# Five feed-forward stages: first weights by plain loads, the others further ahead

## The chip, the cores and the metric

One core of a Trainium2 chip runs the kernel. The metric is the device time of one execution, in microseconds (us). An engine's instructions run in the order in which the program issues them; the engines are PE (matrix products), DVE (vector operations), ACT (activations and copies), POOL (GpSimd) and SP (which issues most of the DMAs).

## The reference

Two network blocks on x of 512 tokens by 1024 features, in float32. What the change touches are the five feed-forward stages; each reads the normed residual stream and adds to it (factor 0.5 in the first four, 1.0 in the fifth). Between them lie the two mixers of the first block and the mixer of the second, which stay as they are.

```python
def _swiglu(x, w_gate, w_up, w_down):
    hid = jax.nn.silu(jnp.einsum('bsd,df->bsf', x, w_gate)) * jnp.einsum('bsd,df->bsf', x, w_up)
    return jnp.einsum('bsf,fd->bsd', hid, w_down)

for l in range(DEPTH):            # DEPTH = 2
    h = h + 0.5 * _swiglu(_rmsnorm(h, ffn1_norm[l]), ffn1_w_gate[l], ffn1_w_up[l], ffn1_w_down[l])
    h = h + _hybrid_mixer(_rmsnorm(h, mix_norm[l]), ...)
    h = h + 0.5 * _swiglu(_rmsnorm(h, ffn2_norm[l]), ffn2_w_gate[l], ffn2_w_up[l], ffn2_w_down[l])
# second block: a mixer, then h = h + (silu(gate) * up) @ w_ffn_out, then the final norm
```

D_MODEL is 1024 and D_FF 2816, so a stage has 22 hidden blocks of 128 for gate and 22 for up.

## The kernel before

**Data.** The residual stream lies transposed in SBUF as eight tiles `h0` to `h7` of 128x512 (features by tokens). For float32 accuracy each operand is split into a high and a low part, `split` or `parts_of`: ACT copies the source to fp32r (`...h`, `whi`), DVE subtracts (`...l`, `wlo`). Each product of a weight and an x tile is then three matmuls.

**A feed-forward stage** (`ffn`, L508) is made in pairs of hidden blocks, 22 pairs, gate and up in turn. A pair of output blocks by pairs of input blocks is a 2x2 matrix product, and it is done with seven products `a` to `g` (`product`, L451) instead of eight, with sums of weight tiles and of x tiles: `halves` (L420) makes the x operands in four blocks (each from two h tiles: on ACT `xe`, `sq`, `bh`, `nh`, `xo`, `sq`, `nh`, `bh`, `th`), and `prepare` (L391) the weights. One product is 12 matmuls of 128x256: 4 blocks, three each. `steps` (L489) gives the order of the products: both products that need only the first weights, a and c, lead each pair. Three PSUM banks per pair, `pX`, `pW`, `pV`, hold a-d-e-g, c-f and b.

**Weights.** A pair's four 128x512 tiles a11, a21, a22, a12 lie side by side in `wq`, a quad. `load_quad` (L378) loads columns 0 to 1023 into `wsum`, 0 to 511 into `wa` and 1024 to 2047 into `wrest`, all from SP, and then POOL issues a DMA that adds columns 512 to 1535 onto `wsum`: its halves become a11+a21 (for e) and a21+a22 (for c). It must wait for the plain `wsum` to land. The sum for d is made by POOL (`ws`, L406), those for f by DVE (L411). `wsum`, `wrest` and the split tiles of 128x1024 share a pool of 12 buffers (`wpool`) with the streamed weights of the mixers and of the down products (`wraw`, split to `whi` and `wlo`); the tiles of 128x512 are in a pool of 63 (`slots`).

**When.** Quads are loaded, and products prepared, LEAD = 8 products ahead in the program (L531). The first two quads of a stage are loaded by `ahead` (L499) before the stage begins: in the constructor for stage 0, in the last quarter of a mixer or of the feed-forward stage before for the others. A scheduler fixes each engine's order of instructions at build time; buffers and semaphores then decide when each one runs. The down products (`pd`, L241 to L243, matmuls of 128x512) of a part of the hidden blocks are run twice within a stage (ENDS), after pairs 3 and 7 of gate and up, and a third time at its end; L526 adds their result to h.

## Time and profile before

| | us |
|---|---|
| median of three runs | 3457.65 (3455.81 to 3466.18) |
| profiled execution | 3456.21 |
| its span | 3454.4 |
| around the span | 1.8 |
| PE busy | 3201.6 |
| DVE busy | 2445.0 |
| ACT busy | 1535.8 |
| POOL busy | 703.2 |

The span is the time from the first instruction to the last. "Busy" leaves out waiting. In a list of waits a row names the waiting engine and tile, and the instruction that came last of those it waited for; in a timeline the bracket behind an instruction gives the idle time before it and what ended that. The mean granted clock of PE is 0.972 of full speed over the run.

### The profile page before, as it was taken

How to read it: one execution, taken by the hardware profiler on the slowest of the kernel's cores; microseconds unless marked ns; L12 is line 12 of the kernel's file. 1: busy time of each engine (PE TensorE's matmuls, PEld its weight loads, DVE VectorE, ACT ScalarE, POOL GpSimd, SP SyncE). 2: the span in 40 equal slices, each digit the busy share in tenths (PEclk: the TensorE clock that was granted, in tenths of full speed). 3: DMA queues.
4: the chain of work that ended last, by engine and by line, in shares of the span. 5: the costliest groups of instructions: out<-in, count | busy, mean ns of one | idle time of the engine just before them, and what ended most of it. 6: DMA issues, size and time to landing. Idle time of an engine off the chain costs nothing. (4 is left out here: it accounts for less than half of the span.)

```text
span 3454.4 us, 48230 instructions
## 1 busy us (share of the span) xinstructions
PE 3201.6 (93%) x18602; PEld 2757.8 (80%) x18602; DVE 2445.0 (71%) x4094; ACT 1535.8 (44%) x2586; POOL 703.2 (20%) x799
## 2 busy tenths in 40 slices
PE   4999999987999799999899799999999999999999
PEld 4998877767998698887777698887777777879888
DVE  6855778657765785767866685667788887568565
ACT  5533534335533453434333453355444366355343
POOL 2211124212111121111431221122111133122111
PEclk9999999998999899999999899999999999999999
DMA  5655332124654374533222274533333222347452
GB/s 141 172 143 136 94 96 75 45 86 104 162 147 125 104 177 130 149 100 98 72 60 82 74 181 133 145 89 107 92 98 104 87 81 74 115 116 177 130 148 83
DMA packets 142470, 391.39 MB, mean 113 GB/s; under 512 B 22176, under 2 KB 38688, under 8 KB 142240
## 3 DMA queue, kind: packets, MB, share of 16 engines
q1 hardware_dynamic: 126400, 330.64, 31.1%
q0 software_dynamic: 15840, 57.68, 10.1%
q8 instruction: 145, 2.38, 0.3%
q14 instruction: 85, 0.70, 0.1%
HBM read 384.85 MB, written 2.88 MB: 112 GB/s over the span
## 5 line engine op out<-in xcount | busy, mean ns | idle before, releaser
L203 DVE TENSOR_TENSOR wlo<-wraw,whi 128x1024 fp32r<-128x1024 f32 x306 | 389.7, 1278 | 117.7 <-ACT whi L202 60.5
L202 ACT ACTIVATE whi<-wraw 128x1024 fp32r<-128x1024 f32 x306 | 320.7, 1052 | 325.2 <-DMA wraw<-ws 293.7
L241 PE MATMUL pd<-hidh,whi 128*128 128x512 f32 x880 | 348.4, 396 | 8.6 <-ACT whi L202 8.6
L243 PE MATMUL pd<-hidh,wlo 128*128 128x512 f32 x880 | 348.2, 396 | 1.2 <-DVE wlo L203 1.2
L242 PE MATMUL pd<-hidl,whi 128*128 128x512 f32 x880 | 347.9, 395 | 0.0
L526 DVE SCALAR_TENSOR_TENSOR h<-pd,h 128x512 f32<-128x512 f32 x120 | 82.7, 689 | 343.2 <-PE pd L243 343.1
L406 POOL TENSOR_TENSOR ws<-wsum,wrest 128x512 f32<-128x512 f32 x110 | 173.7, 1582 | 649.3 <-DMA wsum<-wq 355.3
L465 PE MATMUL pX<-th,whi 128*128 128x256 f32 x880 | 251.4, 286 | 5.4 <-DVE oq L480 3.7
L465 PE MATMUL pX<-tl,whi 128*128 128x256 f32 x880 | 249.4, 283 | 0.0
L465 PE MATMUL pX<-th,wlo 128*128 128x256 f32 x880 | 249.1, 283 | 0.0
L388 POOL DMA_DIRECT2D wsum<-wq x110 | 96.7, 879 | 718.5 <-DMA wsum<-wq 553.4
L241 PEld LDWEIGHTS pd<-hidh,whi 128*128 128x128 f32 x880 | 166.1, 189 | 45.6 <-ACT whi L202 9.0
L243 PEld LDWEIGHTS pd<-hidh,wlo 128*128 128x128 f32 x880 | 166.0, 189 | 40.9 <-DVE wlo L203 2.9
L243 PE MATMUL pj<-x,wlo 128*128 128x512 f32 x476 | 192.8, 405 | 5.9 <-DVE wlo L203 5.9
L242 PEld LDWEIGHTS pd<-hidl,whi 128*128 128x128 f32 x880 | 166.1, 189 | 37.2
L243 PE MATMUL pj<-xh,wlo 128*128 128x512 f32 x476 | 191.5, 402 | 3.2 <-DVE wlo L203 3.2
L241 PE MATMUL pj<-x,whi 128*128 128x512 f32 x476 | 193.2, 406 | 0.8 <-ACT whi L202 0.4
L241 PE MATMUL pj<-xh,whi 128*128 128x512 f32 x476 | 191.1, 401 | 3.1 <-ACT whi L202 3.1
L242 PE MATMUL pj<-xl,whi 128*128 128x512 f32 x476 | 190.4, 400 | 2.0 <-DVE xl L307 2.0
L242 PE MATMUL pj<-x,whi 128*128 128x512 f32 x476 | 191.5, 402 | 0.0
L202 ACT ACTIVATE whi<-wsum 128x1024 fp32r<-128x1024 f32 x110 | 115.6, 1051 | 162.6 <-DMA wsum<-wq 162.6
L203 DVE TENSOR_TENSOR wlo<-wsum,whi 128x1024 fp32r<-128x1024 f32 x110 | 146.9, 1336 | 50.3 <-ACT whi L202 49.7
(456 smaller groups left out, 9643.4 us busy)
## 6 DMA issues: line engine op xcount, KB each, us to landing
wraw<-ws SPq DMA_DIRECT2D x306, 512.0 KB
wsum<-wq SPq DMA_DIRECT2D x110, 512.0 KB
wrest<-wq SPq DMA_DIRECT2D x110, 512.0 KB
wsum<-wq POOLq DMA_DIRECT2D x110, 512.0 KB, 7.3
wa<-wq SPq DMA_DIRECT2D x110, 256.0 KB
csb<-drow SPq DMA_DIRECT2D x32, 256.0 KB
bc<-drow SPq DMA_DIRECT2D x24, 256.0 KB
tab<-tables SPq DMA_DIRECT2D x15, 256.0 KB
```

Of the source, the lines that this page charges most:

```text
L202: self.nc.scalar.activation(hi, src, AF.Copy)
L203: self.nc.vector.tensor_tensor(lo, src, hi.bitcast(F32), ALU.subtract)
L241: nc.tensor.matmul(ps, lhsT=wh, rhs=xh, start=st, stop=False)
L242: nc.tensor.matmul(ps, lhsT=wh, rhs=xl, start=False, stop=False)
L243: nc.tensor.matmul(ps, lhsT=wl, rhs=xh, start=False, stop=en)
L388: nc.gpsimd.dma_start(w.sums, src[:, 512:1536], accum_op=ALU.add)
L406: nc.gpsimd.tensor_tensor(w.s2, w.sums[:, lo], w.rest[:, lo], ALU.add)
L465: nc.tensor.matmul(ps, lhsT=a[:, j * P:(j + 1) * P], rhs=b, start=p in "acb" and j + i == 0, stop=j == len(xs) - 1 and i == 2, skip_group_ ...
L526: nc.vector.scalar_tensor_tensor(self.h[mm], pds[mm], factor, self.h[mm], ALU.mult, ALU.add)
```

## The change

The first two quads of each stage are loaded as four plain tiles of 256 KB each (`early_tile`, into `slots`) in place of the plain and the accumulating DMAs; DVE adds what has to be summed (`prepare_early`), and each of the seven weights is split by itself. Other quads are loaded 16 products ahead, prepared 8 ahead as before. In the constructor, h tiles and weight tiles alternate in order of use, a small tile of gains (`gain0`) comes first, and cols and the constants come behind. The first two pairs of stage 0 begin with a, c and b together, block of x by block of x (`opening`), 72 matmuls. `ealog` is made in the first mixer. The 110 accumulating DMAs become 100.

```diff
--- before.py
+++ after.py
@@ -158,17 +158,19 @@
         self.tiny = pool("tiny", 4)
         self.psum = pool("psum", 1, space=bass.MemoryType.PSUM)
         self.dram = pool("dram", 2, space=bass.MemoryType.DRAM)
+        self.gain0 = self.const.tile([P, KB], F32, name="gain0")
+        nc.sync.dma_start(self.gain0, a["cols"][:, 0:KB])
+        self.h = [self.hpool.tile([P, S], F32, name=f"h{k}") for k in range(KB)]
+        self.ahead(start=True)
+        g, u = self.first
+        for t in ("h0", (g, 0), (u, 0), "h2", (g, 1), (g, 2), "h4", (u, 1), (u, 2), "h6", "h1", (g, 3), "h3", (u, 3), "h5", "h7"):
+            if isinstance(t, str):
+                k = int(t[1:])
+                nc.sync.dma_start(self.h[k], a["xT"][:, k])
+            else:
+                self.early_tile(*t)
         self.cols = self.const.tile([P, NCOL], F32, name="cols")
         nc.sync.dma_start(self.cols, a["cols"])
-        self.ealog = self.const.tile([P, DEPTH + 1], F32, name="ealog")
-        nc.scalar.activation(self.ealog, self.cols[:, COLS["alog"]:COLS["alog"] + DEPTH + 1], AF.Exp)
-        self.h = []
-        for k in range(KB):
-            t = self.hpool.tile([P, S], F32, name=f"h{k}")
-            nc.sync.dma_start(t, a["xT"][:, k])
-            self.h.append(t)
-            if k == 1:
-                self.ahead()
         self.cst = self.const.tile([P, len(CONSTS), P], F32, name="cst")
         nc.sync.dma_start(self.cst, a["consts"])
 
@@ -179,6 +181,8 @@
         return self.c(name).unsqueeze(1).to_broadcast([P, n, P])
 
     def col(self, name, i=0, rows=slice(0, P)):
+        if name == "ffn1_0":
+            return self.gain0[rows, i:i + 1]
         j = COLS[name] + i
         return self.cols[rows, j:j + 1]
 
@@ -388,11 +392,39 @@
         nc.gpsimd.dma_start(w.sums, src[:, 512:1536], accum_op=ALU.add)
         return w
 
+    def load_early(self, key):
+
+        q = len(self.quads)
+        self.quads.append(key)
+        return type("Early", (), dict(raw={}, src=self.a["wq"][q], part={}, s={}))
+
+    def early_tile(self, w, i):
+        w.raw[i] = self.slot("wr")
+        self.nc.sync.dma_start(w.raw[i], w.src[:, 512 * i:512 * i + 512])
+
+    def prepare_early(self, w, p):
+        add = lambda name, a, b: (w.s.setdefault(name, self.slot("ws")), self.nc.vector.tensor_tensor(w.s[name], a, b, ALU.add))[0]
+        a11, a21, a22, a12 = (w.raw[i] for i in range(4))
+        if p == "c":
+            t = add("c", a21, a22)
+        elif p == "d":
+            t = add("d", w.s["c"], a11)
+        elif p == "e":
+            t = add("e", a11, a21)
+        elif p == "f":
+            self.prepare(w, "d")
+            t = add("f", a12, w.s["d"])
+        else:
+            t = {"a": a11, "b": a12, "g": a22}[p]
+        w.part[p] = self.split(t, "we")
+
     def prepare(self, w, p):
 
         nc = self.nc
         if p in w.part:
             return
+        if hasattr(w, "raw"):
+            return self.prepare_early(w, p)
         lo, hi = slice(0, 512), slice(512, 1024)
         if p == "a":
             w.part["a"] = self.split(w.a11, "wa")
@@ -448,22 +480,37 @@
             xs.append(x)
         return xs, acc
 
+    def matmuls(self, m, p, j, x, last):
+
+        bank = "X" if p in "adeg" else "W" if p in "cf" else "V"
+        if p in "acb" and j == 0:
+            m.ps[bank] = self.ps(f"p{bank}", tag="mm" if bank == "X" else "mx")
+        wh, wl = m.w.part[p]
+        xh, xl = x[p]
+        for i, (a, b) in enumerate(((wh, xh), (wh, xl), (wl, xh))):
+            self.nc.tensor.matmul(m.ps[bank][:, 0:HT], lhsT=a[:, j * P:(j + 1) * P], rhs=b, start=p in "acb" and j + i == 0,
+                                  stop=last and i == 2, skip_group_check=True)
+
+    def opening(self, ms, ps, xs):
+
+        for j, x in enumerate(xs):
+            for p in ps:
+                for m in ms:
+                    self.matmuls(m, p, j, x, j == len(xs) - 1)
+        for p in ps:
+            for m in ms:
+                self.taken(m, p)
+
     def product(self, m, p, xs):
 
 
-        nc = self.nc
-        self.prepare(m.w, p)
-        wh, wl = m.w.part[p]
-        bank = "X" if p in "adeg" else "W" if p in "cf" else "V"
-        if p in "acb":
-            m.ps[bank] = self.ps(f"p{bank}", tag="mm" if bank == "X" else "mx")
+        for j, x in enumerate(xs):
+            self.matmuls(m, p, j, x, j == len(xs) - 1)
+        self.taken(m, p)
+
+    def taken(self, m, p):
+        nc = self.nc
         X, W, V = (m.ps[b][:, 0:HT] if b in m.ps else None for b in "XWV")
-        ps = m.ps[bank][:, 0:HT]
-        for j, x in enumerate(xs):
-            xh, xl = x[p]
-            for i, (a, b) in enumerate(((wh, xh), (wh, xl), (wl, xh))):
-                nc.tensor.matmul(ps, lhsT=a[:, j * P:(j + 1) * P], rhs=b, start=p in "acb" and j + i == 0,
-                                 stop=j == len(xs) - 1 and i == 2, skip_group_check=True)
         lo, hi = slice(0, HT), slice(HT, S)
         if p == "a":
             m.snap = self.slot("snap")
@@ -486,21 +533,30 @@
             nc.vector.scalar_tensor_tensor(o[:, lo], X, -1.0, m.r[:, lo], ALU.mult, ALU.mult)
             nc.vector.scalar_tensor_tensor(o[:, hi], m.o2[:, hi], -1.0, m.r[:, hi], ALU.mult, ALU.mult)
 
-    def steps(self, n):
+    def steps(self, n, first):
 
         s = lambda *t: [(i, p) for i, ps in t for p in ps]
-        yield s((0, "ac"), (1, "ac"), (0, "db"), (1, "d"), (0, "e"))
-        yield s((2, "ac"), (0, "fg"), (1, "eb"), (2, "d"), (1, "fg"))
+        if first:
+            yield [(i, p) for p in "acb" for i in range(2)]
+            yield s((0, "d"), (1, "d"), (0, "e"), (2, "ac"), (0, "fg"), (1, "e"), (2, "d"), (1, "fg"))
+        else:
+            yield s((0, "ac"), (1, "ac"), (0, "db"), (1, "d"), (0, "e"))
+            yield s((2, "ac"), (0, "fg"), (1, "eb"), (2, "d"), (1, "fg"))
         for i in range(3, n):
             yield s((i, "ac"), (i - 1, "eb"), (i, "d"), (i - 1, "fg"))
         yield s((n - 1, "be"))
         yield s((n - 1, "fg"))
 
-    def ahead(self):
+    def ahead(self, start=False):
 
         names, l = FFNS[self.stage]
         self.stage += 1
-        self.first = [self.load_quad((names[i], l, 0)) for i in range(2)]
+        self.first = [self.load_early((names[i], l, 0)) for i in range(2)]
+        if start:
+            return
+        for i in range(4):
+            for w in self.first:
+                self.early_tile(w, i)
         for p in "ac":
             for w in self.first:
                 self.prepare(w, p)
@@ -512,10 +568,11 @@
         for m, w in zip(pairs, self.first):
             m.w = w
         self.first = None
-        steps = list(self.steps(n))
+        start = gain == "ffn1_0"
+        steps = list(self.steps(n, start))
         flat = [t for s in steps for t in s]
         xs, acc = self.halves(gain)
-        done, hid, part, due = 0, [], [], None
+        done, hid, part, due, r = 0, [], [], None, None
 
         def down(blocks, ks, first=True, last=True):
             for mm in blocks:
@@ -527,12 +584,18 @@
 
         pds = {}
         for k, step in enumerate(steps):
+            if start and k == 0:
+                for i, p in step:
+                    self.prepare(pairs[i].w, p)
+                self.opening(pairs[:2], "acb", xs)
+                done, step = len(step), []
             for i, p in step:
-                for j, q in flat[done:done + LEAD]:
+                for j, q in flat[done:done + 2 * LEAD]:
                     if pairs[j].w is None:
                         pairs[j].w = self.load_quad(pairs[j].key)
+                for j, q in flat[done:done + LEAD]:
                     self.prepare(pairs[j].w, q)
-                if done == 4:
+                if r is None and done >= 4:
                     r = self.slot("R")
                     self.rsqrt(r, self.total(acc), 1.0 / DM, self.slot)
                     for m in pairs:
@@ -662,6 +725,9 @@
 
     def mixer1(self, l, nxt):
         nc = self.nc
+        if l == 0:
+            self.ealog = self.const.tile([P, DEPTH + 1], F32, name="ealog")
+            nc.scalar.activation(self.ealog, self.cols[:, COLS["alog"]:COLS["alog"] + DEPTH + 1], AF.Exp)
         xs, r, total = self.norm(f"mix_{l}")
         m = type("Mix", (), dict(l=l, xs=xs, r=r, y=[]))
         ps = self.proj(("small", l), xs)
```

**Place 1: ACT at the start of stage 0.** Before, from its first weight: `wah` and `whi` are the first two quads' weights, `xe` to `th` the x blocks.

```order
L253 ACTIVATE wah_97<-wa_84 128x512
L202 ACTIVATE whi_105<-wsum_83 128x1024
L253 ACTIVATE wah_101<-wa_91 128x512
L435 ACTIVATE xe_129<-h0_79,cols_75 128x512
L313 ACTIVATE sq_140<-h0_79 128x512
L417 ACTIVATE bh_127<-xe_129 128x256
L202 ACTIVATE whi_109<-wsum_90 128x1024
L417 ACTIVATE nh_133<-n_131 128x256
L440 ACTIVATE xo_130<-h1_81,cols_75 128x512
```

Now, from the middle of the first x block: 

```order
L449 ACTIVATE nh_119<-n_117 128x256
L472 ACTIVATE xo_116<-h1_78,gain0_75 128x512
L317 ACTIVATE sq_134<-h1_78 128x512
L730 ACTIVATE ealog_3984<-cols_109 128x3
L449 ACTIVATE nh_119<-n_117 128x256
L449 ACTIVATE bh_123<-xo_116 128x512
```

the second half of the second x block:

```order
L472 ACTIVATE xo_148<-h3_80,gain0_75 128x512
L317 ACTIVATE sq_168<-h3_80 128x512
L206 ACTIVATE whi_407<-wsum_371 128x1024
L449 ACTIVATE nh_151<-n_149 128x256
L449 ACTIVATE bh_155<-xo_148 128x512
L206 ACTIVATE whi_538<-wsum_378 128x1024
L449 ACTIVATE th_153<-t_150 128x512
L467 ACTIVATE xe_183<-h4_81,gain0_75 128x512
```

and the end of the fourth:

```order
L449 ACTIVATE th_223<-t_220 128x512
L257 ACTIVATE weh_251<-wr_86 128x512
L257 ACTIVATE weh_255<-wr_88 128x512
L257 ACTIVATE weh_261<-ws_259 128x512
L257 ACTIVATE weh_267<-ws_265 128x512
L257 ACTIVATE weh_271<-wr_102 128x512
```

The first two quads' weights (now `weh`) stood ahead of and inside the first x block and now stand behind the fourth. `ealog`, which reads cols, stands in the first block, and two `whi` of the third and fourth quads (wsum_371, wsum_378) in the second.

**Place 2: DVE where the first part's down products begin in stage 0** (`h0` is the first result added to h; the `wlo<-wrest` next to it belongs to a product f). Before:

```order
L548 TENSOR_TENSOR o_1507<-o_1507,o_1645 128x512
L526 SCALAR_TENSOR_TENSOR h0_79<-pd_1710,h0_79 128x512
L203 TENSOR_TENSOR wlo_1597<-wsum_1570,whi_1596 128x1024
L254 TENSOR_TENSOR wdl_1651<-ws_1648,wdh_1650 128x512
L203 TENSOR_TENSOR wlo_1669<-wrest_1434,whi_1668 128x1024
L486 SCALAR_TENSOR_TENSOR o_1646<-pX_1443,R_361 128x256
```

Now:

```order
L533 SCALAR_TENSOR_TENSOR o_1681<-pX_1478,R_427 128x256
L207 TENSOR_TENSOR wlo_1632<-wsum_1443,whi_1631 128x1024
L611 TENSOR_TENSOR o_1542<-o_1542,o_1680 128x512
L207 TENSOR_TENSOR wlo_1704<-wrest_1313,whi_1703 128x1024
L258 TENSOR_TENSOR hidl_1744<-o_1542,hidh_1743 128x512
L611 TENSOR_TENSOR o_1543<-o_1543,o_1681 128x512
L258 TENSOR_TENSOR hidl_1749<-o_1543,hidh_1748 128x512
L583 SCALAR_TENSOR_TENSOR h0_77<-pd_1752,h0_77 128x512
L258 TENSOR_TENSOR wal_2003<-wa_1584,wah_2002 128x512
```

Both `wlo` of the pairs in work stood behind the addition to h0 and now stand ahead of it. The nine other places of this kind (two in each stage) differ in the same way.

**Place 3: ACT at the start of the third stage (ffn1 of layer 1, from about 1150 us)**, behind the stage before it; `whi<-wraw` are weights of that stage's last down products. Before, from within the first x block on:

```order
L417 ACTIVATE nh_11269<-n_11267 128x256
L202 ACTIVATE whi_11163<-wsum_11141 128x1024
L417 ACTIVATE th_11271<-t_11268 128x512
L202 ACTIVATE whi_11167<-wsum_11148 128x1024
L435 ACTIVATE xe_11297<-h2_113,cols_75 128x512
L313 ACTIVATE sq_11308<-h2_113 128x512
L417 ACTIVATE bh_11263<-xe_11297 128x256
L417 ACTIVATE nh_11301<-n_11299 128x256
L440 ACTIVATE xo_11298<-h3_115,cols_75 128x512
L313 ACTIVATE sq_11318<-h3_115 128x512
L417 ACTIVATE nh_11301<-n_11299 128x256
L202 ACTIVATE whi_11174<-wraw_11172 128x1024
```

Now, from the last weights ahead of the first x block on:

```order
L257 ACTIVATE weh_11219<-wr_11201 128x512
L257 ACTIVATE weh_11225<-ws_11223 128x512
L206 ACTIVATE whi_11238<-wraw_11236 128x1024
L257 ACTIVATE weh_11231<-ws_11229 128x512
L467 ACTIVATE xe_11329<-h0_77,cols_109 128x512
L317 ACTIVATE sq_11340<-h0_77 128x512
L449 ACTIVATE bh_11327<-xe_11329 128x256
L206 ACTIVATE whi_11270<-wraw_11268 128x1024
L449 ACTIVATE nh_11333<-n_11331 128x256
L472 ACTIVATE xo_11330<-h1_78,cols_109 128x512
```

The `whi` of two down products stood in the second and third x blocks, behind `whi` that wait for accumulates, and now stand ahead of the first block and inside it; the four `weh` of the first two quads' a and c stand ahead of the x blocks.

## Rows read from the trace of the kernel before

**Rows 1.** the page, parts 1 (busy us, share, instructions) and 6 (us to landing)

```profile
PE 3201.6 (93%) x18602; PEld 2757.8 (80%) x18602; DVE 2445.0 (71%) x4094; ACT 1535.8 (44%) x2586; POOL 703.2 (20%) x799
...
wsum<-wq POOLq DMA_DIRECT2D x110, 512.0 KB, 7.3
```

**Rows 2.** PE's waits, whole run: engine, line, awaited instruction: us, times, longest

```profile
PE pX L465 <- ACT bh L417: 53.8, 6, 21.4
PE pV L465 <- ACT wbh L253: 23.2, 5, 5.3
PE pW L465 <- DVE wlo L203: 22.4, 15, 2.0
...
PE pd L241 <- ACT whi L202: 10.6, 2, 8.6
```

**Rows 3.** PE's timeline, 160 to 172 us: start, us, instruction, [idle before <- releaser]

```profile
171.13 0.38 PE L465 MATMUL pW<-bh,wlo 128*128 128x256 f32 x1 [2.00 <-DVE wlo L203]
```

**Rows 4.** DVE's timeline, 160 to 173 us

```profile
167.52 0.69 DVE L526 SCALAR_TENSOR_TENSOR h<-pd,h 128x512 f32<-128x512 f32 x1 [3.78 <-PE pd L243]
168.13 1.22 DVE L203 TENSOR_TENSOR wlo<-wsum,whi 128x1024 fp32r<-128x1024 f32 x1
169.26 0.68 DVE L254 TENSOR_TENSOR wdl<-ws,wdh 128x512 fp32r<-128x512 f32 x1
169.86 1.22 DVE L203 TENSOR_TENSOR wlo<-wrest,whi 128x1024 fp32r<-128x1024 f32 x1
```

**Rows 5.** PE's timeline, 0 to 64 us

```profile
21.39 0.79 PE L465 MATMUL pX<-bh,wah 128*128 128x256 f32 x2 [21.39 <-ACT bh L417]
...
63.05 0.39 PE L465 MATMUL pX<-th,whi 128*128 128x256 f32 x1 [0.35 <-ACT snap L472]
```

**Rows 6.** ACT's timeline, 0 to 66 us

```profile
18.32 1.06 ACT L202 ACTIVATE whi<-wsum 128x1024 fp32r<-128x1024 f32 x1 [8.70 <-DMA wsum<-wq]
...
19.80 0.71 ACT L435 ACTIVATE xe<-h,cols 128x512 f32<-128x512 f32 x1
...
27.81 0.71 ACT L435 ACTIVATE xe<-h,cols 128x512 f32<-128x512 f32 x1
...
37.36 0.71 ACT L435 ACTIVATE xe<-h,cols 128x512 f32<-128x512 f32 x1
...
45.73 0.71 ACT L435 ACTIVATE xe<-h,cols 128x512 f32<-128x512 f32 x1
...
55.27 0.63 ACT L417 ACTIVATE th<-t 128x512 fp32r<-128x512 f32 x1 [3.89 <-DVE t L446]
```

**Rows 7.** POOL's timeline, 0 to 60 us

```profile
8.63 1.00 POOL L388 DMA_DIRECT2D wsum<-wq  x1 [8.18 <-DMA wsum<-wq]
...
50.08 4.54 POOL L406 TENSOR_TENSOR ws<-wsum,wrest 128x512 f32<-128x512 f32 x3
```

**Rows 8.** busy us (count) of PE, PEld, DVE, ACT, POOL; clock, DMA share, GB/s

```profile
15.00:20.00 5.00, 0.00 (x0) 0.00 (x0) 0.59 (x1) 1.68 (x3) 0.00 (x0) 1.00 1.06 252
20.00:25.00 5.00, 3.12 (x11) 2.62 (x12) 3.89 (x7) 4.24 (x9) 0.85 (x1) 1.00 1.02 399
55.00:63.00 8.00, 5.61 (x24) 5.11 (x24) 4.64 (x7) 3.90 (x8) 0.00 (x0) 0.57 0.00 0
63.00:75.90 12.90, 12.85 (x108) 12.85 (x108) 8.52 (x14) 10.53 (x18) 0.88 (x1) 1.00 0.55 124
```

**Rows 9.** ACT's timeline, 1150 to 1204 us

```profile
1153.62 0.72 ACT L435 ACTIVATE xe<-h,cols 128x512 f32<-128x512 f32 x1 [5.76 <-DVE h L526]
...
1165.00 1.06 ACT L202 ACTIVATE whi<-wsum 128x1024 fp32r<-128x1024 f32 x1 [3.55 <-DMA wsum<-wq]
...
1190.17 1.06 ACT L202 ACTIVATE whi<-wsum 128x1024 fp32r<-128x1024 f32 x1 [3.64 <-DMA wsum<-wq]
...
1198.76 0.63 ACT L417 ACTIVATE th<-t 128x512 fp32r<-128x512 f32 x1 [5.49 <-DVE t L446]
```

**Rows 10.** PE's timeline, 1150 to 1216 us

```profile
1171.18 0.79 PE L241 MATMUL pd<-hidh,whi 128*128 128x512 f32 x1 [8.61 <-ACT whi L202]
```

## What the change does to the time: the prediction

> **What bounds the kernel now.** I read the page first: PE is busy 3201.6 us of the 3454.4 us span [rows 1], so 252.8 us of idle PE are all that better loading could return. The list of PE's waits over the whole run then says whom it idles for [rows 2]. Look there for two kinds. Four of the rows belong to the openings of the five feed-forward stages: `bh`, an operand half of x, costs 53.8 us in 6 waits; `wbh`, the first weight after the x blocks, 23.2 us in 5; a `whi` of a down product 10.6 us in 2. The fourth kind is in mid-stage: products on bank W wait for `wlo`, 22.4 us in 15 waits, none above 2.0 us.
>
> The timelines tell what these waits are. In mid-stage, PE stands 2.00 us at 171.13 us [rows 3]. The reason is on DVE [rows 4]: it stood 3.78 us for the last matmul of the first down block (`h<-pd` at 167.52), and three subtractions lay behind it in its order, two `wlo` and a `wdl`; the `wlo` that PE wants comes last, from 169.86 to 171.08. This is a matter of order on DVE; no transfer is late by then. It happens where a part's down products begin, twice in each stage: 10 x 2.0 = 20.0 us of the 22.4 us, which leaves 2.4 us for five small ones.
>
> In stage 0, PE begins at 21.39 us and reaches the eighth product (84 matmuls done) at 63.05 [rows 5]. Between the two, ACT paces it [rows 6]: it first stands 8.70 us for a summed weight tile, then passes the four x blocks, which begin at 19.80, 27.81, 37.36 and 45.73, and the last `th` comes at 55.27: 8.0 to 9.5 us a block.
>
> **The change part by part.** *Order at a part's first down product.* Loading 16 products ahead leaves the scheduler a summed tile early enough to put its subtractions before the addition to h: in the new DVE order both `wlo` stand ahead of `h0`, and the same in all ten places. In the new order the second `wlo` follows the end of a pX product by four DVE instructions, 0.4 + 1.22 + 0.68 + 1.22 = 3.5 us by like rows [rows 4]; PE has 24 matmuls of 128x512 and 12 of 128x256 to do meanwhile, 36 x 0.119 us at the least = 4.3 us (the 0.119 below). So nothing should be late. Between 0 and all of it, I take **-20 us**; bounds -22.4 and 0.
>
> *Stage 0.* The first weights now come plainly, without the accumulate that took from 8.63 [rows 7] to 18.32 us [rows 6]. But ACT's new order does not use that. `ealog` stands inside the first x block and waits for cols, which is queued behind sixteen tiles of 256 KB: 4.2 MB at the 252 to 399 GB/s of these microseconds [rows 8] are 10.5 to 16.6 us, so about 12 to 18 us from the start; I take 17, since the two first x rows must share with weights. Two `whi` of the third and fourth quads stand in the second block and wait for accumulates that are issued behind all this: plain tiles at about 21 us, then 7.3 (the median landing [rows 1]) to 9.7 us each; I take 30 and 36 us. Blocks three and four follow at 8.0 to 9.5 us each, and all six first weights come after the last `th`. So the last `th` comes at about 36 + 1.7 + 2 x 8.4 = 54.5, as late as before (55.27), and PE's first matmul moves from 21.39 to about 55 us. The opening's 72 matmuls were half done by then before. Now they run after it: the first 28 at a low clock (0.57 granted in 55 to 63 us, mostly the lower of its two levels, 1.2 GHz: 0.21 us each), the rest at 12.85 us / 108 = 0.119 us [rows 8]: 28 x 0.21 + 44 x 0.119 = 11 us, to 66. Twelve more bring the eight-product mark to 67.5 against 63.05. Behind it the sums c+a11 and their like are new DVE work: for each of d, d, e, f, e, f an addition and a subtraction of 128x512, 2 x 0.68 us [rows 4], beside about 0.5 us of evictions, 1.9 us where PE needs 12 x 0.119 = 1.4; with a first gap of some 2.5 us this costs 4 to 5 us more. **+9 us**. The low bound is -5 (cols and both accumulates early: the blocks end about 14 us sooner, but the weights' chain remains), the high bound +20 (each accumulate lands 9.7 us after the one before it has landed).
>
> *The stage after ffn2_0 (from 1150 us).* ACT took the blocks at 1153.62 and stood 3.55 us and 3.64 us for accumulated tiles, then 5.49 us before the last `th` at 1198.76 [rows 9]; behind the first of these waits stood the `whi` of a down product, and PE lost 8.61 us at 1171.18 [rows 10]. In the new order the down weights come before the x blocks. But four `weh` come before them too, and the last waits for a DVE addition that stands behind the h3 addition, so the first block begins about 6 us later, near 1160. Four blocks of 8.0 to 8.5 us and two `whi` of 1.05 us make 1194 to 1196. **-4 us**; bounds -8.6 (the whole PE wait) and +3.
>
> *The other three openings* follow a mixer. The down weights gain a few us, the `whi` of the third quad now stands in front of or inside the x blocks and loses them again: **0**, each -3 to +3. Ten quads less for POOL's accumulates and first sums, 40 additions of 0.68 us more on DVE (27 us over the run, busy 2445.0 of 3454.4 us): nothing outside the openings, since PE is the bound there; without that cover they would cost those 27 us. The rewritten product function issues the same matmuls.
>
> Sum: -20 + 9 - 4 = -15 us. From the profiled execution's 3456.2 us this is 3441.2 us. That execution lies 1.4 us under the median of the three runs (3457.65), so 3441 to 3443; I say **3442**.
>
> **The rivals.** *The stalls stay* (the change does not do what it says). The loads stand earlier in the program, but the twelve w buffers are still twelve; if a tile waits for its buffer until PE has left the quad two before, `wlo` comes as late as now. Then only +9 - 4 remain: 3461 us. For it: the new waits of the first summed tiles are on the end of a pX product. Against it: from that end to the tile's first use PE has 182 matmuls in the new order, 182 x 0.119 = 21.7 us, and 145 or fewer before.
>
> *Slower: ACT stands behind accumulates at each opening.* More bytes are wanted in the same microseconds: two early quads, and in front of or inside the x blocks a third and a fourth quad of 1.75 MB each. If both hoisted `whi` wait as two did here, 3.55 and 3.64 us [rows 9], four stages lose 7.2 us each; stage 0 loses the +20 of its bound. 4 x 7.2 + 20 - 20 = +29: 3485 us. It decides at the moment when ACT reaches the fourth quad's `whi`, about 18 us into the blocks: if the accumulate has landed, nothing is lost. For it: in 15 to 25 us the DMA engines were full (share 1.02 to 1.06, [rows 8]) and the accumulate took 9.7 us and not 7.3. Against it: at the later openings ACT's own blocks give it those 18 us. The Trainium skill, DMA: Bandwidth & Descriptors, section Issuing engines are not separate DMA queues, says that transfers from any issuer end up on the same 16 engines and interleave; by that rule the sixteen tiles put first slow the accumulates of the next quads, which is this rival's side.
>
> *Faster still: the last block loses its POOL neighbour.* Before the last `th`, ACT waited 3.89 us in stage 0 [rows 6] and 5.49 us in the later stage [rows 9]; POOL ran three sums `ws` then, 4.54 us from 50.08 on [rows 7], and two of the three belong to the first quads, which DVE now adds itself, later. If their neighbourhood is what stretched DVE's part, 2 to 3.5 us come back at each of five openings: -13 more, 3429 us. I kept it out of the sum, since the same sums return as DVE additions behind `th`. The Trainium skill, SBUF — State Buffer, section Who interferes with whom, has the rule for it: a DVE instruction with two SBUF inputs contends with a GpSimd instruction that reads SBUF. By that rule the gain is real wherever no other POOL sum moves into the place.
>
> **How the numbers follow.** My forecast has 0.58, with 3431 to 3452 from the bounds of its smaller terms; the stalls that stay 0.15; slower 0.12; faster still 0.15. 0.3% of the median is 10.4 us, about what a measurement of this kernel can tell from no change: faster means under 3447.3, slower over 3468.0. Of the forecast's own band four fifths lie under that, so faster has 0.58 x 0.8 + 0.15 = 0.61, same 0.58 x 0.2 + 0.15 = 0.27, slower 0.12. The range reaches from the faster rival's 3425 to just over the 3461 of the stalls that stay: 3425 to 3464; it leaves out the slower rival and the tail of the faster one.
>
> **What would show it.** Right: in the profile after, no wait of 2.0 us on `wlo` in mid-stage, and DVE's `h0` addition behind both `wlo`; PE's first matmul at 50 to 58 us, with `ealog` and two `whi<-wsum` on ACT waiting for transfers before it; no 8.6 us wait on `whi` near 1170. Wrong: `wlo` still in the list with some 20 us; a first matmul before 40 us; or ACT waits on `wsum` of over 3 us at the openings from 800 us on, which would be the slower rival. The sum would be wrong too if PE's wait on the d, e, f weights behind the first 72 matmuls were over 8 us.

## The result and the profile after: slower by 0.55%

The changed kernel takes 3477.51 us (median of 9 runs, 3469.14 to 3489.38) against 3459.31 us of the kernel before on the same chips; the ratio is 1.0055, 95% interval 1.0041 to 1.007. The forecast was 3442. The profiled execution has a span of 3477.7 us against 3454.4.

The page's first part, busy us and share. The same 18602 matmuls are busy 14.4 us longer than before [rows 1]:

```profile
PE 3216.0 (92%) x18602; PEld 2762.9 (79%) x18602; DVE 2489.4 (72%) x4144; ACT 1554.5 (45%) x2606; POOL 659.7 (19%) x779
```

So of the 23.3 us of span, 14.4 are slower matmuls and 8.9 more idle time. The list of PE's waits over the whole run (us, times, longest) shows where the idle time is now:

```profile
PE pX L491 <- ACT weh L257: 52.8, 5, 50.2
PE pd L245 <- ACT whi L206: 32.3, 10, 3.7
PE pX L491 <- ACT bh L449: 20.3, 6, 4.7
...
PE pX L491 <- DVE oq L527: 11.2, 28, 1.0
PE pd L247 <- DVE wlo L207: 10.2, 18, 2.0
...
PE pW L491 <- DVE wlo L207: 2.3, 4, 0.6
```

The `wlo` waits of [rows 2] fell from 22.4 us to 2.3, as forecast. But there are now ten waits for `whi`, the high part of a down product's weights, 2.8 to 3.7 us each. In place of 53.8 us for `bh` PE waits 50.2 us once for the first `weh` of stage 0.

The new wait at the first part of stage 0. PE's timeline (start, us, instruction, idle before and releaser):

```profile
182.90 0.50 PE L245 MATMUL pd<-hidh,whi 128*128 128x512 f32 x1 [3.21 <-ACT whi L206]
183.24 0.40 PE L246 MATMUL pd<-hidl,whi 128*128 128x512 f32 x1
184.16 0.50 PE L247 MATMUL pd<-hidh,wlo 128*128 128x512 f32 x1 [0.53 <-DVE wlo L207]
...
185.18 0.63 PE L247 MATMUL pd<-hidh,wlo 128*128 128x512 f32 x1
185.60 0.63 PE L245 MATMUL pd<-hidh,whi 128*128 128x512 f32 x1
```

SP's timeline ahead of it, and ACT's copy that PE waits for:

```profile
173.89 0.33 SPq L389 DMA_DIRECT2D wsum<-wq  x1
174.78 0.33 SPq L391 DMA_DIRECT2D wrest<-wq  x1
175.20 0.38 SPq L215 DMA_DIRECT2D wraw<-ws  x1
```

```profile
181.79 1.06 ACT L206 ACTIVATE whi<-wraw 128x1024 fp32r<-128x1024 f32 x1 [5.58 <-DMA wraw<-ws]
```

The second unit of down weights (`wraw`, 512 KB) is issued straight behind two tiles of a quad that is not needed for 16 products, and is in use, that is copied by ACT, 6.6 us later (175.20 to 181.79). The other nine places have the same row of three on SP, with 6.2 to 7.1 us from the unit's issue to ACT's copy. In the kernel before the row was the same, but each of the three found a buffer in time, and ACT copied the unit without waiting:

```profile
151.70 0.33 SPq L385 DMA_DIRECT2D wsum<-wq  x1
156.16 0.33 SPq L387 DMA_DIRECT2D wrest<-wq  x1
159.84 0.33 SPq L211 DMA_DIRECT2D wraw<-ws  x1
```

```profile
173.52 1.04 ACT L202 ACTIVATE whi<-wraw 128x1024 fp32r<-128x1024 f32 x1
```

Part of the later issue is stage 0's later opening. Measured from DVE's first addition to h (167.52 before, 176.33 now), the unit was issued 7.7 us ahead of it before and 1.1 us ahead of it now. SP's list of waits in the change, 168 to 176 us, shows why all three come late and together: SP stood 9.0 us until the subtraction `wlo` had given a buffer of the pool free.

```profile
SPq L389 <- DVE wlo L207: 9.0, 1, 9.0
```

The stall has a second price. PE in windows of 5 us from the end of each of the ten waits (busy us and count, clock, DMA share, GB/s); four of the ten:

```profile
182.90:187.90 5.00, 4.47 (x12) 0.68 0.43 138
...
1079.91:1084.91 5.00, 4.96 (x11) 0.50 0.39 129
...
2226.09:2231.09 5.00, 4.96 (x11) 0.50 0.36 123
...
3356.95:3361.95 5.00, 4.47 (x13) 0.71 0.49 149
```

All ten lie between 0.50 and 0.71, partly or wholly at the lower level of 1.2 GHz: a matmul of 128x512 starts every 0.43 us (185.18, 185.60) instead of every 0.23. Summed over the ten windows, (1 - clock) x 5 us, an estimate of what the lower clock took, is 18.6 us, beside 32.3 us of idle time: 50.8 us, rounded at the end. The same sum for the kernel before, with windows of 4 us behind its ten `wlo` waits, of which three:

```profile
171.13:175.13 4.00, 4.00 (x19) 0.57 0.60 174
...
1315.41:1319.41 4.00, 3.24 (x22) 1.00 0.47 177
...
2208.74:2212.74 4.00, 3.91 (x18) 0.57 0.64 194
```

Seven of these ten lie at 0.57 to 0.68 and three at 1.00, 11.4 us lost beside 20.0 us of idle time: 31.4 us. (Windows of 10 us for both kernels give 21.6 and 13.7 us in place of 18.6 and 11.4, about the same difference.) So the ten places cost 19.4 us more than before, where the forecast had 20 us less.

### The profile page after: what moved, and what is told of

It is laid out like the page before. It is cut to its first block, busy times and chain, and to the rows that moved or that the text cites. A ratio compares the mean times of both kernels' runs of the same rounds, so it can differ in the third digit from the quotient of the medians.

```text
span 3477.7 us, 48303 instructions
## 1 busy us (share of the span) xinstructions
PE 3216.0 (92%) x18602; PEld 2762.9 (79%) x18602; DVE 2489.4 (72%) x4144; ACT 1554.5 (45%) x2606; POOL 659.7 (19%) x779
## 4 chain that ended last, share of the span: by engine, by line
PE 57%; DVE 20%; ACT 8%; issue 7%; DMA 5%; POOL 3%; SPq 0%; DVEq 0%; ACTq 0%; POOLq 0%
PE pX L491 10%; PE pd L247 8%; PE pd L245 8%; PE pd L246 7%; DVE wlo L207 4%; PE pW L491 4%; PE pj L247 3%; PE pj L246 3%; PE pj L245 3%; DMA wraw<-ws 3%; PE pV L491 2%; ACT whi L206 1%; DVE wbl L258 1%; DVE wrest L443 1%; PE pt L641 1%
## 5 line engine op out<-in xcount | busy, mean ns | idle before, releaser
L245 PE MATMUL pd<-hidh,whi 128*128 128x512 f32 x880 | 355.8, 404 | 32.3 <-ACT whi L206 32.3
L247 PE MATMUL pd<-hidh,wlo 128*128 128x512 f32 x880 | 356.9, 406 | 8.5 <-DVE wlo L207 8.2
L438 POOL TENSOR_TENSOR ws<-wsum,wrest 128x512 f32<-128x512 f32 x100 | 158.2, 1582 | 542.1 <-PE pd L247 413.8
L392 POOL DMA_DIRECT2D wsum<-wq x100 | 87.9, 879 | 832.7 <-PE pX L491 392.3
L491 PE MATMUL pX<-th,whi 128*128 128x256 f32 x800 | 228.5, 286 | 11.4 <-DVE oq L527 11.2
L491 PE MATMUL pX<-th,wlo 128*128 128x256 f32 x800 | 224.8, 281 | 0.0
L491 PE MATMUL pX<-tl,whi 128*128 128x256 f32 x800 | 224.2, 280 | 0.0
L207 DVE TENSOR_TENSOR wlo<-wsum,whi 128x1024 fp32r<-128x1024 f32 x100 | 166.7, 1667 | 34.4 <-ACT whi L206 31.3
L491 PEld LDWEIGHTS pX<-th,whi 128*128 128x128 f32 x800 | 150.8, 189 | 19.2 <-DVE oq L527 17.8
```

The costliest lines, as they stand in the source:

```text
L207: self.nc.vector.tensor_tensor(lo, src, hi.bitcast(F32), ALU.subtract)
L245: nc.tensor.matmul(ps, lhsT=wh, rhs=xh, start=st, stop=False)
L247: nc.tensor.matmul(ps, lhsT=wl, rhs=xh, start=False, stop=en)
L392: nc.gpsimd.dma_start(w.sums, src[:, 512:1536], accum_op=ALU.add)
L438: nc.gpsimd.tensor_tensor(w.s2, w.sums[:, lo], w.rest[:, lo], ALU.add)
L491: self.nc.tensor.matmul(m.ps[bank][:, 0:HT], lhsT=a[:, j * P:(j + 1) * P], rhs=b, start=p in "acb" and j + i == 0, stop=last and i == 2, s ...
```

## The experiments

Each kernel was compared with the kernel before on the same chip, five rounds each. Two theories stood at first. **A**: the second unit is late because SP has a quad's loads ahead of it. **B**: the pool of twelve buffers is too small at this place, whatever the order. (The expectations call this A2 in e5 and e6 and B from e9 on; in e1 and e2 their B is another rival, that the early plain loads cost the time.) A mark below is the start of one of DVE's additions to h in a kernel's trace, less the same in the kernel before; positive is later. A stage's end is its last addition, or, in the second stage, which the third follows at once, the first addition of its last part.

**Which part of the change costs? The lead.** e1 is the change with loads 8 ahead, e2 the kernel before with 16:

```diff
 e1_lead8 (the change):
-                for j, q in flat[done:done + 2 * LEAD]:
+                for j, q in flat[done:done + LEAD]:
 e2_only16 (before), prepared in a loop of its own, 8 ahead:
-                for j, q in flat[done:done + LEAD]:
+                for j, q in flat[done:done + 2 * LEAD]:
```

> The changed kernel with its quads loaded 8 products ahead again; early loads and stage 0 as changed. Theory A (the loads 16 ahead put an extra quad in front of the down products' second weight unit on SP, which makes PE wait 3.2 us for whi in each of ten places): these ten waits go, the stage-by-stage marks stop drifting by about 4.8 us a stage, total about 24 us under the changed kernel, 3452 to 3457 us, ratio to before 0.998 to 1.000. Theory B (the early plain loads, with their DVE sums, cost the time in mid-stage too): no change, 3472 to 3480 us, ratio 1.004 to 1.006.

> The kernel before with nothing changed but the loads 16 products ahead. Theory A: the ten waits on whi appear here as well, in place of the ten of 2.0 us on wlo; about 24 us over before, 3480 to 3486 us, ratio 1.006 to 1.008. Theory B: within 5 us of before, ratio 0.998 to 1.002.

e1: 3471.33 us, ratio 1.0049 (1.0035 to 1.0063); the `whi` waits are gone and the `wlo` waits back, 21.1 us in 14, as A said, but A's time (0.998 to 1.000) did not come. By the marks the stretches from a stage's first addition to its end are 17 us shorter in e1 than in the change; the mixers win 8 us less, and the openings lose 3 us more. e2: 3483.51 us, 1.0083 (1.0068 to 1.0097), with 34.4 us in 13 waits on `whi`, in time and waits about as A said: the lead alone makes them.

**The opening of stage 0.** e3 has the constructor and first stage of before; e4 prepares a and c of the first two pairs ahead of the x blocks:

```diff
 e4_weights_first (the change, in ffn, ahead of halves):
+        if start:
+            for p in "ac":
+                for m in pairs[:2]:
+                    self.prepare(m.w, p)
```

> The changed kernel with the constructor and stage 0 of before (accumulating loads there, no opening); early loads in the other four stages and the loads 16 ahead stay. Both theories: the 9 to 10 us that stage 0 lost up to its first down part come back, 3466 to 3470 us, ratio 1.002 to 1.004. If stage 0 were not what its marks say: 3475 us or more.

> The changed kernel with the a and c weights of stage 0 prepared ahead of the x blocks in the program. If PE's late start (50.2 us) comes from ACT's order: PE starts at 18 to 24 us, behind cols and the first x block, and stage 0 ends 6 to 10 us sooner, 3467 to 3472 us, ratio 1.0025 to 1.004. If the x blocks alone set the pace of the opening (last th at 49 us): PE starts early but ends the opening at most 3 us sooner, 3474 to 3478 us.

e3: 3474.17 us, 1.0051 (1.0037 to 1.0064), over its expected range; the medians do not tell it from the change, and only its trace shows the opening, by a first mark of +3.3 us where the change has +8.8. e4: 3477.66 us, 1.0064 (1.005 to 1.0078): PE begins at 19.29 us and not at 50.20, and nothing is won, since it then waits for each block and, as in the change, for the later sums:

```profile
81.93 0.58 PE L491 MATMUL pW<-bh,weh 128*128 128x256 f32 x1 [4.88 <-ACT weh L257]
```

**Early loads alone.** e7 has them in the four later stages with 8 ahead and stage 0 of before; e8 only in the second and the fourth, which follow mixers 0 and 1:

```diff
 e8_after_mixers (e7, in ahead):
-        if self.stage == 1:
+        if self.stage not in (2, 4):
             self.first = [self.load_quad((names[i], l, 0)) for i in range(2)]
```

> The early plain loads alone, in the four later stages: stage 0 of before, loads 8 ahead. If the costs seen so far add up (run with 8 ahead: +17 us on before, of it 9.5 in stage 0): +8 us, ratio 1.001 to 1.004, with 4 to 7 us lost at the openings of the second, fourth and fifth stage and 4 at the third, and 6 to 8 us gained in each mixer of the first block. Rival: the early loads cost nothing by themselves and stage 0 is the whole loss: ratio 0.997 to 1.000.

> Early plain loads only at the second and fourth stage, those behind the mixers of the first block; everything else as before. If the mixers' gain is from these loads (they leave the w buffers to the mixer's last weights): gain of 6 to 8 us in each mixer against 4 to 7 us lost at each opening; 0 to 8 us under before, ratio 0.997 to 1.000. Rival: the mixers' gain came from elsewhere, then only the losses are left: +8 to +13 us, ratio 1.002 to 1.004.

e7: 3470.95 us, 1.0036 (1.0023 to 1.0048), in its range. e8: 3462.37 us, 1.001 (1.0001 to 1.002), between its two ranges. The marks show each of them faster through the first block's mixers (7.8 and 4.2 us in the first) and slower at the openings behind (7.0 and 6.1 us at the second stage).

**The second unit earlier; a lead of 12.**

```diff
 e5_unit_early (the change):
                 self.load_unit(len(self.keys) // UNIT)
+                self.load_unit(len(self.keys) // UNIT + 1)
 e6_lead12 (before):
-                for j, q in flat[done:done + LEAD]:
+                for j, q in flat[done:done + 12]:
```

> The changed kernel (16 ahead, early loads, new stage 0) with the second weight unit of each mid-stage group of down products asked for together with the first, so that on SP it stands before the last quad's two loads. Theory A (the wait on whi comes from the place of that unit in SP's order): the ten waits of 3.2 us on whi shrink to under 1 us each, and the 2.0 us waits on wlo do not come back; 20 to 30 us under the changed kernel, about 3450 us, ratio 0.997 to 1.000. Rival A2 (the twelve w buffers are short when quads are loaded 16 ahead, whoever stands first on SP): the wait moves to the next unit or to a quad, total within 8 us of the changed kernel, ratio 1.003 to 1.006.

> The kernel before with its loads 12 products ahead in place of 8. Theory A: the extra quad is then asked for before the second unit in some groups only or not at all; between before and the run with 16 ahead, ratio 1.000 to 1.004, with either the 2.0 us waits on wlo or the 3.2 us waits on whi at each group but not both. Rival A2: in proportion to the lead, ratio 1.003 to 1.005.

e5: 3494.26 us, 1.0103 (1.0089 to 1.0116), against theory A as it then stood and over A2's range too: the second unit came in time, the third took its place, and `whi` cost 45.3 us in 14 waits. SP and ACT there:

```profile
180.78 0.33 SPq L389 DMA_DIRECT2D wsum<-wq  x1
182.24 0.33 SPq L391 DMA_DIRECT2D wrest<-wq  x1
182.67 0.37 SPq L215 DMA_DIRECT2D wraw<-ws  x1
```

```profile
189.42 1.06 ACT L206 ACTIVATE whi<-wraw 128x1024 fp32r<-128x1024 f32 x1 [10.35 <-DMA wraw<-ws]
```

Again 6.7 us from issue to use behind a `wsum` and a `wrest`. e6: 3501.1 us, 1.0122 (1.0109 to 1.0136), the worst and over both ranges, so the price does not grow with the lead alone. Its largest new waits are PE's on `snap`, 64.9 us in 31, because ACT stands on an accumulated tile ahead of `snap`:

```profile
107.71 1.06 ACT L202 ACTIVATE whi<-wsum 128x1024 fp32r<-128x1024 f32 x1 [6.98 <-DMA wsum<-wq]
```

**Order against buffers.** e9 keeps 16 ahead but asks for no quad beyond 8 in the step that ends with the down products; e10 holds back for two steps; e11 has all quads 16 ahead and one buffer more; e12 is before with that buffer.

```diff
 e9_hold_one (e2, one line):
-                for j, q in flat[done:done + 2 * LEAD]:
+                for j, q in flat[done:done + (2 * LEAD if due is None or k != due else LEAD)]:
 e10_hold_two: k > due in place of k != due
 e11_lead16_13w, e12_before_13w:
-SLOTS = 63
-WBUFS = 12
+SLOTS = 62
+WBUFS = 13
```

> The kernel before with quads 16 products ahead, except in the step that ends with a part's down products: there only 8 ahead, so that in SP's order the second down unit follows the first directly and no wsum and wrest stand between them. Theory A (SP's order: the unit is late because SP stands on a wsum that waits for a buffer): the ten waits pd<-whi of some 3 us and the wlo waits of 2.0 us are both gone, PE's list shows pd<-whi under 12 us in all, ratio to before 0.995 to 1.000. Theory B (twelve buffers are too few at this place whatever the order): the unit waits for its buffer itself, pd<-whi stays at 25 us or more, ratio 1.005 to 1.009.

> As the run before, but the 16 are held back to 8 from the end of a part's last pair on, two steps instead of one, so that two quads less stand ahead of the down units. Theory A: like the run before, 0.995 to 1.000, as the second unit is already next in SP's order there. Theory B: two quads less in the pool free up to six of the twelve buffers, so this one is better than the run before by 10 us or more, 0.996 to 1.001.

> The kernel before with all quads 16 products ahead and 13 w buffers in place of 12 (62 slots in place of 63). SP's order at the first part is unchanged: wsum, wrest, then the second unit. Theory B: one buffer more lets SP issue the wsum earlier by the time of one buffer's turn; pd<-whi falls from 34 us to under 15, ratio 1.000 to 1.004. Theory A in its strict form (order alone): pd<-whi stays at 25 to 35 us, 1.006 to 1.009.

> Control: the kernel before with 13 w buffers and 62 slots, loads 8 ahead. At a part's first down products DVE's order is as before (h0, then wlo, wdl, wlo), so the ten waits of 2.0 us on wlo stay; ratio 0.998 to 1.002 by both theories.

e9: 3431.74 us, **0.9929** (0.9915 to 0.9942). e10: 3446.8 us, 0.9966 (0.9952 to 0.9979). e11: 3473.36 us, 1.0045 (1.0032 to 1.0058). e12: 3445.24 us, 0.9969 (0.9958 to 0.9981). The waits on `whi` of e9 and of e11:

```profile
PE pd L241 <- ACT whi L202: 16.0, 12, 3.4
```

```profile
PE pd L241 <- ACT whi L202: 45.2, 11, 5.5
```

One held quad gives 1.5% against e2; a buffer more takes none of the waits away. (In e11 SP issues the second unit at 168.42 us, but again behind a `wsum` and a `wrest`, at 163.12 and 167.63, and behind an accumulate that POOL issued at 167.34; ACT copies it at 176.85.) e9 went under A's range, with 16.0 us of `whi` waits where A had under 12; e10 did worse than e9 where both theories had it as good or better, and why was not followed. e11 missed both ranges: it is faster than e2, by the marks in the mixers and not inside the stages. The control e12 missed too: its `wlo` waits stay (22.8 us), and the 13 us come from elsewhere (10.6 us in the first mixer, 10.8 in the second, by the marks).

**The change with that line alone; with the other parts undone.** e13 is the change with e9's line, e14 is e9 with 13 buffers, e15 is e13 with the constructor and first stage of before.

> The changed kernel with one line different: in the step that ends with a part's down products quads are requested only 8 products ahead, so that SP has the second down unit directly behind the first. Theory A (the whole mid-stage loss is SP's order at ten places): pd<-whi falls from 32.3 us to under 18, the marks of the five stages no longer drift up between the first and the second part, stage 0's opening keeps its +9; ratio to before 0.991 to 0.996. Rival (what the plain first loads cost elsewhere eats it): whi waits go, but the openings of the four later stages still cost 3 to 5 us each, ratio 0.997 to 1.001.

> The kernel before with the held 16 (as e9_hold_one) and 13 w buffers. If the two gains stand apart (25 us from SP's order and wlo, 13 us from the buffer in mixers and openings): ratio 0.988 to 0.991. If the held order already gives what the buffer gave: 0.992 to 0.994. If the buffer changes the scheduler's order for the worse again, as it did with all quads 16 ahead: above 0.995.

> The changed kernel with the held 16 (as e13_after_hold) and with the constructor and the first stage of the kernel before (accumulating loads, blocks of x as before); the early loads stay in the four later stages. If the new opening of stage 0 costs the 9 us of the prediction's term, this is 6 to 10 us faster than e13_after_hold at the first part's h1 mark and at the end: ratio 0.988 to 0.990. If the opening's loss is taken back within the stage: ratio 0.990 to 0.993, as e13_after_hold. As to order alone: pd<-whi stays under 18 us either way.

e13: 3426.75 us, **0.9912** (0.9899 to 0.9926). e14: 3426.78 us, 0.9911 (0.9898 to 0.9925). e15: 3420.2 us, **0.9885** (0.9868 to 0.9901), the lowest median, though its interval overlaps those of e13 and e14. e13 and e15 lie in the first of their expected ranges, e14 between its first two. The line alone, in e9, has 0.9929 (0.9915 to 0.9942), which overlaps e13's interval: what the early loads add to it is not shown, and e14 has e13's time without them.

e13's place in stage 0, on SP, ACT and PE:

```profile
174.51 0.33 SPq L215 DMA_DIRECT2D wraw<-ws  x1
```

```profile
178.24 1.06 ACT L206 ACTIVATE whi<-wraw 128x1024 fp32r<-128x1024 f32 x1 [1.40 <-DMA wraw<-ws]
```

```profile
179.34 0.50 PE L245 MATMUL pd<-hidh,whi 128*128 128x512 f32 x1 [1.24 <-ACT whi L206]
```

and SP's wait, 168 to 176 us:

```profile
SPq L215 <- DVE wlo L207: 12.7, 1, 12.7
```

This corrects both theories. The unit is hardly issued earlier (174.51 against 175.20): with quads 16 ahead in the pool it waits for the same `wlo` and a buffer, as B has it. What A has right is who goes first when buffers come free: ahead of the quad the unit is in use 3.7 us after its issue (3.6 to 4.3 at the ten places), behind `wsum` and `wrest` after 6.6. That is 2.9 us here; PE's wait fell by 2.0 us here (3.21 to 1.24), and over the ten places from 32.3 us to 12.8:

```profile
PE pd L245 <- ACT whi L206: 12.8, 10, 1.8
```

At 1.24 us of idle time the clock stays up; e13 in the same windows as above, three of ten:

```profile
179.34:184.34 5.00, 5.00 (x24) 1.00 0.19 55
...
1433.89:1438.89 5.00, 5.00 (x17) 0.66 0.15 32
...
3304.78:3309.78 5.00, 5.00 (x24) 1.00 0.19 43
```

Nine stand at 1.00; the tenth, behind the longest wait (1.79 us), at 0.66. The ten places cost 12.8 + 1.7 = 14.5 us, 36.4 less than in the change. The spans differ by 53.2 us; by the marks 48 of them lie between the first addition and the end of the five stages, so the line works there and not in the mixers or the openings. Of the 17 us beyond the ten places, smaller waits on `oq` and `wlo` gave 6; the rest was not followed. The scheduler also made a new order on DVE and PE for e13, so the line changes more than SP's row; no run has SP's order alone.

## Why the prediction was wrong

Measured by the profiles, each a single execution. The first two rows are sums over PE's waits and clock, the others marks:

| part | forecast us | measured us |
|---|---|---|
| ten part boundaries, idle and clock | -20 | +19.4 |
| waits on `oq` and small `wlo` of down products | 0 | about +12 |
| opening of stage 0 | +9 | +8.8; e13 less e15: 5.6 |
| stage after ffn2_0, opening | -4 | +0.3 |
| other three openings | 0 | +4.8, +5.6, +2.8 |
| mixers 0 and 1, mixer 2 | 0 | -11.6, -11.5, +1.5 |

The first two rows also hold waits that lie in the openings, so the column is not a sum. By the marks alone the openings lose 22.2 us, the stretches from a stage's first addition to its end 22.6, and the mixers win 21.6: +23.1 us of the span's 23.3. Why the waits on `oq` and the small ones on `wlo` grew is open.

**Order at a part's first down product: the step that failed.** That the `wlo` waits would go was right, and why: in the new DVE order both `wlo` run ahead of `h0`, without a wait. "So nothing should be late" was wrong. The step asked what stands behind `h0` on DVE and whether PE has work for 3.5 us; it did not ask what the quads loaded earlier take from the other user of the same pool and queue. The next thing late was the second unit: it was issued 1.1 us ahead of the first addition to h where before it was 7.7, and it got the DMA engines behind a quad. In place of -20 us the ten places gave +19.4. The prediction saw the buffers (in "the stalls stay") and the moment when ACT meets late transfers (in the slower rival), but put the one in the place of the old wait and the other at the openings. The time went the slower rival's way, not by its path: ACT's only wait of over 3 us on a `wsum` at the openings from 800 us on is one of 3.18 at 1185.87 us, where before two of 3.55 and 3.64 stood [rows 9].

**The price of a stall.** The -20 counted idle time alone. The waits it removed cost 31.4 us with the clock, the new ones 50.8; an answer with the right wait and its idle time only would still have been off by 7 us.

**Stage 0.** The sum was near by luck. Both summed tiles came earlier than taken (`whi` at 29.01 and 31.42 us, forecast 30 and 36), the last `th` at 49.00 and not 54.5, PE's first matmul at 50.20 (forecast range 50 to 58); the opening's 72 matmuls took 11.1 us, as forecast. The prediction also misread its mark: at 63.05 us PE had done 72 matmuls of the products (two a, two c, a b and a d) and begun the first e; 84 were done at 64.58. The change had 84 done at 63.99, so nothing was lost up to there, where the prediction had 4.5 us. All of the +8.8 came behind it, where it had 4 to 5: one wait of 4.89 us at 82.32 for a sum, and smaller ones. Nor is all of it the new opening: with the old opening and loads 16 ahead, e3's first mark is +3.3 and e2's +2.3. (In its first paragraph the prediction counts four rows of waits at the openings and names three.)

**The stage after ffn2_0** went as forecast in its rows: no 8.6 us wait near 1170. But other waits took its place, on `bh` (3.21 and 4.53 us at 1193.72 and 1202.14) and `weh` (3.14 us at 1210.88), so from the second part's last addition to the next stage's first PE's idle time fell only from 19.9 to 17.3 us, and the mark shows no gain; the -4 did not come. **The other openings** lost 13 us, and the mixers won 21.6; neither was in the sum. In the mixers the waits of 5.0 and 5.3 us for `o` ahead of a transpose are 0.7 us each in the change, so DVE has it sooner there; that the early tiles lie in slots and leave the w buffers free for the mixers' weights fits e12, which won 10.6 us in the first mixer by a buffer, but no run tells these apart.

**Transfers on the same engines.** At the first boundary a `wraw` of SP took 3.7 us ahead of a quad, 6.6 behind two of its tiles, and 8.4 in e11 behind a tile and an accumulate issued by POOL. The Trainium skill, DMA: Bandwidth & Descriptors, section Issuing engines are not separate DMA queues, has all transfers on the same 16 engines; these rows fit, though only e11's has a second issuer. At stage 0's start, where the prediction weighed it, the accumulates were not slowed: the first three landed after 8.5, 6.4 and 5.6 us in the change, 9.7, 8.8 and 5.6 before.

**Faster still** had a true mechanism. With no `ws` sum of POOL beside the last x block of stage 0, ACT's wait for the last `th` fell from 3.89 us [rows 6] to 1.50. It won nothing, as the weights stand behind it.

## What to carry to other kernels

When loads are moved ahead, read the order on the queue that issues them and ask which more urgent load now waits for their buffers and stands behind them: here the gain came with the order, and one line that held back a quad's loads at ten places turned +0.55% into -0.9%. Price a PE stall with the matmuls that follow it, not by its idle time alone. A static order can come out worse at 12 ahead than at 8 or 16, so try the neighbours and look where each stands in line.

## What the runs showed of the hardware

- The clock behind a stall: after PE's idle times of 1.10 to 1.43 us it stayed at 1.00 in all nine places of e13, after 1.79 us it showed 0.66, after ten of 2.79 to 3.74 us in the change 0.50 to 0.71. After 2.0 us in the kernel before it fell in seven places of ten.
- The clock row does not tell all. Behind the change's 50.20 us of idle time at the start it shows 1.00 for 50 to 54 us, yet most matmuls of 128x256 start 0.21 us apart there, and 0.12 us apart from 55 us on.
- A load of 512 KB was in use 3.6 to 4.3 us after its issue at e13's ten places, with 256 KB issued 0.4 us behind it; 6.2 to 7.1 us at the change's ten places, behind 1 MB issued within 1.4 us before.
- DVE beside POOL: in the kernel before, POOL's three sums run from 50.08 to 54.62 us. DVE's `bl<-xo` of 128x512 takes 1.75 us beside them, and the same instruction in the change, with POOL idle, 0.69:

```profile
51.75 1.75 DVE L418 TENSOR_TENSOR bl<-xo,bh 128x512 fp32r<-128x512 f32 x1
```

```profile
47.60 0.69 DVE L450 TENSOR_TENSOR bl<-xo,bh 128x512 fp32r<-128x512 f32 x1 [0.16 <-ACT bh L449]
```

The Trainium skill, SBUF — State Buffer, section Who interferes with whom, has DVE instructions with two SBUF inputs contend with GpSimd instructions that read SBUF, as POOL's sums do; these two rows agree.
